# Rotary embedding on one core: the first slab's load in one piece instead of eight, and the stores issued by GpSimd's software ring instead of ScalarE's hardware ring

## The chip, the core and the metric

The kernel runs on one core of a Trainium2 chip. The time is device microseconds (us) of one execution of the whole program. The profile comes from one further execution under the hardware profiler, with its own time.

## The reference

The kernel applies rotary position embedding to `x`, shape (16, 512, 1024) in float32, seen as 16 heads of 64 numbers. With `x1` and `x2` the two halves of a head and `cos`, `sin` of shape (512, 32), shared by all batches and heads:

```python
x = x.reshape(batch, seq, num_heads, head_dim)
x1, x2 = x[..., :half_dim], x[..., half_dim:]
rotated = concatenate([x1 * cos - x2 * sin,
                       x1 * sin + x2 * cos], axis=-1)
```

Input and output are 33.55 MB each, so 67.1 MB pass through the DMA engines, plus 0.13 MB of tables.

## The kernel before, in words

The 16 batches are cut into eight **slabs** of two batches. A slab is 128 partitions by 8192 float32, so one partition holds one contiguous run of 32 KB in HBM, and one slab is 4.19 MB. Five slab buffers (`slots = 5`) lie in SBUF. Slab `s + 5` is loaded into the buffer of slab `s`, once the store of slab `s` has landed.

All loads are issued by SyncE (SP), in its hardware ring: slabs 1 to 7 by `load` (L62), each as one DMA over 128 partitions. The first slab is loaded by a loop of its own (L68): eight DMAs, and DMA number `p` writes partitions p, p+8, p+16 and so on, 16 of them, 32 KB each. GpSimd (POOL) issues the two table loads (L78) in its software ring and builds a selection matrix. TensorE and VectorE (DVE) make from it a bfloat16 table `tab` in which cos and sin stand in the order of the slab.

The work is done in **passes**. For slabs 0 to 5 a pass is the whole slab; slabs 6 and 7 are cut into two passes of half a slab. Below, 6a and 6b are the halves of slab 6, and 7a and 7b those of slab 7. A pass has these steps:

1. ScalarE (ACT) casts the slab to bfloat16, `xb` (`cast`, L120). Two `xb` buffers exist.
2. DVE multiplies twice and adds once (L140 twice, L143); the products with sin go into the slab's own buffer.
3. ACT casts `xb` back to float32 into the slab (L146).
4. After a slab's last pass, ACT issues the store of the whole slab as one DMA (L148), in ACT's own hardware ring. Then the load of slab `s + 5` is put into SP's queue.

The source writes the input cast of pass `i + 1` ahead of the DVE work of pass `i`. The framework's scheduler settles the order on each engine from the program, and each engine runs its queue strictly in order. At the end of this kernel ACT's queue is: input cast 7a, output cast 6b, input cast 7b, store 6, output cast 7a, output cast 7b, store 7.

The framework gives DMAs of the hardware rings eight completion semaphores in turn, and those of the software ring eight others. A DMA whose semaphore is still in use waits at issue until the earlier DMA has landed.

Of the kernel before, what the change touches and what calls it, by code (L numbers as in the profile page):

```python
# [2 lines left out]

# [4 lines left out]


@with_exitstack  # L10
def kernel(
    ctx: ExitStack,
    tc: tile.TileContext,
    x: bass.AP,
    cos: bass.AP,
    sin: bass.AP,
    num_heads: int,
    out: bass.AP,
):
    nc = tc.nc  # L20
    P = nc.NUM_PARTITIONS

    batch, seq, dim = x.shape
    nh = num_heads
    hd = dim // nh
    half = hd // 2
    bf16 = mybir.dt.bfloat16
    f32 = mybir.dt.float32

    nb = 2  # L30
    slots = 5
    nslabs = batch // nb
    rpp = nb * seq // P
    W = rpp * dim
    SP = seq // rpp
    TW = rpp * half

    out_flat = out.rearrange("b s h d -> b s (h d)")

    singles = ctx.enter_context(tc.tile_pool(name="singles", bufs=1))  # L40
    slabs = ctx.enter_context(tc.tile_pool(name="slabs", bufs=slots))
    xpool = ctx.enter_context(tc.tile_pool(name="xpool", bufs=2))
    psum = ctx.enter_context(tc.tile_pool(
        name="psum", bufs=1, space=bass.MemoryType.PSUM))


    def dram(t, s, a=0, n=W):
        return bass.AP(tensor=t.tensor, offset=t.offset + s * nb * seq * dim + a,
                       ap=[[W, P], [1, n]])


    def view(t, offset, *dims):
        return dataclasses.replace(t, offset=t.offset + offset,
                                   ap=[t.ap[0], *[list(d) for d in dims]])


    slab = {}


    def load(s):  # L60
        slab[s] = slabs.tile([P, W], f32, tag="slab", name="slab")
        nc.sync.dma_start(out=slab[s], in_=dram(x, s))  # L62

    slab[0] = slabs.tile([P, W], f32, tag="slab", name="slab")
    for p in range(P // 16):
        nc.sync.dma_start(  # L68
            out=slab[0][p::P // 16, :],
            in_=bass.AP(tensor=x.tensor, offset=x.offset + p * W,  # L70
                        ap=[[P // 16 * W, 16], [1, W]]))


    TR = seq // P
    G = rpp // TR
    raw = singles.tile([P, 2 * TR * half], f32, tag="raw")
    for i, src in enumerate((cos, sin)):
        nc.gpsimd.dma_start(out=view(raw, i * TR * half, (1, TR * half)), in_=bass.AP(  # L78
            tensor=src.tensor, offset=src.offset,
            ap=[[TR * half, P], [1, TR * half]]))  # L80

    for s in range(1, slots):
        load(s)


    pick = singles.tile([P, G * P], bf16, tag="pick")
    nc.gpsimd.memset(pick, 0.0)  # L87
    for g in range(G):
        part = view(pick, g * P, (SP, P // SP), (1, SP))
        nc.gpsimd.affine_select(  # L90
            out=part, in_=part, compare_op=mybir.AluOpType.not_equal, fill=1.0,
            base=-g, pattern=[[0, P // SP], [-G, SP]], channel_multiplier=1)

    tab1 = singles.tile([P, 2 * TR * half], bf16, tag="tab1")
    nc.vector.tensor_copy(out=tab1, in_=raw)  # L95
    acc = psum.tile([P, 2 * TW], f32, tag="acc")
    for i in range(2):
        for g in range(G):
            nc.tensor.matmul(view(acc, i * TW + g * TR * half, (1, TR * half)),  # L99
                             view(pick, g * P, (1, P)),  # L100
                             view(tab1, i * TR * half, (1, TR * half)),
                             start=True, stop=True)

    tab = singles.tile([P, 2 * rpp * hd], bf16, tag="tab")
    nc.vector.tensor_copy(out=view(tab, 0, (hd, 2 * rpp), (1, half)),  # L105
                          in_=view(acc, 0, (half, 2 * rpp), (1, half)))
    nc.vector.tensor_copy(out=view(tab, half, (hd, rpp), (1, half)),  # L107
                          in_=view(acc, 0, (half, rpp), (1, half)))
    nc.vector.tensor_scalar_mul(  # L109
        out=view(tab, rpp * hd + half, (hd, rpp), (1, half)),  # L110
        in0=view(acc, TW, (half, rpp), (1, half)), scalar1=-1.0)

    xb = {}


    def cast(u):
        s, r, n = u
        if r == 0:
            xb[s] = xpool.tile([P, W], bf16, tag="xb", name="xb")
        nc.scalar.copy(out=view(xb[s], r * dim, (1, n * dim)),  # L120
                       in_=view(slab[s], r * dim, (1, n * dim)))

    passes = []
    for s in range(nslabs):
        n = rpp if s < nslabs - 2 else rpp // 2
        passes += [(s, r, n) for r in range(0, rpp, n)]


    cast(passes[0])
    for i, (s, r, n) in enumerate(passes):
        if i + 1 < len(passes):
            cast(passes[i + 1])
        xs = view(slab[s], r * dim, (1, n * dim))
        xu = view(xb[s], r * dim, (1, n * dim))

        t2 = view(slab[s].bitcast(bf16), 2 * r * dim, (1, n * dim))
        for t, a in ((t2, rpp * hd), (xu, 0)):
            nc.vector.tensor_mul(  # L140
                out=t, in0=xu,
                in1=view(tab, a + r * hd, (hd, n), (0, nh), (1, hd)))
        nc.vector.tensor_add(  # L143
            out=xu, in0=xu, in1=view(t2, half, (hd, n * nh), (-half, 2), (1, half)))

        nc.scalar.copy(out=xs, in_=xu)  # L146
        if r + n == rpp:
            nc.scalar.dma_start(out=dram(out_flat, s), in_=slab[s])  # L148
            if s + slots < nslabs:
                load(s + slots)  # L150


# [1 line left out]
_INS = ['x', 'cos', 'sin', 'num_heads']  # L154
_OUTS = [((16, 512, 16, 64), 'float32')]

_NUMBERS = {'num_heads': 16}


# [26 lines left out]
```

## Time and profile before

| | |
|---|---|
| median of 3 runs | 171.97 us (171.81 to 172.14) |
| the profiled execution | 171.81 us, of which the profile's span is 170.0 us |
| ACT busy | 113.5 us (67%) |
| DVE busy | 108.7 us (64%) |
| POOL busy | 2.3 us (1%) |
| DMA | 67.24 MB, mean 395 GB/s over the span |

The span runs from the first instruction to the last event of the program; about 1.8 us of the execution's time lie outside it. The page cuts the span into 40 slices of 4.25 us, and gives for each the busy share of the 16 DMA engines and what they moved. The busy share of an engine's packets says that packets were in work, not how fast; the line of GB/s under it does.

### The profile page before, as it was taken

The page shows a single profiled execution, that of the slowest core. Times are in us where ns is not written, and L with a number is a line of the kernel's source. Part 1 is how long each engine was busy: PE and PEld are TensorE (multiplying, and loading weights), DVE is VectorE, ACT ScalarE, POOL GpSimd, SP SyncE. Part 2 cuts the span into 40 slices and gives each one's busy share as a digit, 9 for nine tenths or more (in the row PEclk, how much of TensorE's full clock was granted, in tenths as well). Part 3 has the DMA queues.
Part 4 walks back from the last instruction along what each step waited for, and adds up shares of the span by engine and source line. Part 5 has one row for each costly group of instructions (what it writes and reads, how often), then busy time and mean ns, then how long its engine had stood idle before and what let it go on. Part 6 is the DMA issues. An engine that isn't in the chain of part 4 may idle for free.

```text
span 170.0 us, 169 instructions
## 1 busy us (share of the span) xinstructions
PE 0.6 (0%) x4; PEld 0.4 (0%) x4; DVE 108.7 (64%) x34; ACT 113.5 (67%) x21; POOL 2.3 (1%) x9
## 2 busy tenths in 40 slices
PE   0010000000000000000000000000000000000000
PEld 0000000000000000000000000000000000000000
DVE  0030000399999889979979997994965959980000
ACT  0000039695298999999999999908999599917000
POOL 5000000000000000000000000000000000000000
DMA  5989979999999999999999898989898989898985
GB/s 133 268 185 193 239 285 455 409 455 409 455 409 455 409 455 432 432 439 424 463 401 478 385 486 378 486 378 486 378 486 378 486 378 486 378 493 378 486 378 239
DMA packets 2480, 67.24 MB, mean 395 GB/s; under 512 B 400, under 2 KB 400, under 8 KB 432
## 3 DMA queue, kind: packets, MB, share of 16 engines
q1 hardware_dynamic: 1264, 33.56, 52.0%
q10 hardware_dynamic: 1152, 33.55, 45.7%
q0 software_dynamic: 64, 0.13, 0.4%
HBM read 33.69 MB, written 33.55 MB: 395 GB/s over the span
## 4 chain that ended last, share of the span: by engine, by line
DMA 42%; ACT 33%; DVE 12%; SPq 2%; issue 2%; ACTq 0%
DMA slab<-in_x_dram 27%; ACT slab L146 17%; ACT xb L120 15%; DMA out_dram<-slab 15%; DVE xb L143 4%; DVE slab L140 4%; DVE xb L140 4%; SPq L68 2%; ACT L120 1%; ACTq L148 0%; ACTq L120 0%; ACTq L146 0%; SPq L62 0%
## 5 line engine op out<-in xcount | busy, mean ns | idle before, releaser
L120 ACT CAST xb<-slab 128x8192 bf16<-128x8192 f32 (+1 forms) x10 | 56.5, 5652 | 10.0 <-DMA slab<-in_x_dram 8.7
L146 ACT CAST slab<-xb 128x8192 f32<-128x8192 bf16 (+1 forms) x10 | 56.5, 5650 | 8.6 <-DVE xb L143 8.6
L140 DVE TENSOR_TENSOR slab<-xb,tab 128x8192 bf16<-128x8192 bf16 (+1 forms) x10 | 35.7, 3571 | 33.0 <-ACT xb L120 32.9
L143 DVE TENSOR_TENSOR xb<-xb,slab 128x8192 bf16<-128x8192 bf16 (+1 forms) x10 | 35.7, 3572 | 0.3
L140 DVE TENSOR_TENSOR xb<-xb,tab 128x8192 bf16<-128x8192 bf16 (+1 forms) x10 | 35.7, 3571 | 0.3
L120 ACT ACT_TABLE_LOAD x1 | 1.3, 1283 | 24.0 <-DMA slab<-in_x_dram 24.0
L95 DVE CAST tab<-raw 128x256 bf16<-128x256 f32 x1 | 0.3, 294 | 9.3 <-DMA raw<-in_sin_dram 9.3
L105 DVE CAST tab<-acc 128x512 bf16<-128x512 f32 x1 | 0.7, 692 | 0.7 <-PE acc L99 0.7
L78 POOL DMA_DIRECT2D raw<-in_cos_dram x1 | 0.7, 674 | 0.8 <-POOLq L167 0.8
L99 PE MATMUL acc<-tab,pick 128*128 128x128 bf16 x4 | 0.6, 299 | 9.6 <-DVE tab L95 9.6
L78 POOL DMA_DIRECT2D raw<-in_sin_dram x1 | 0.5, 534 | 0.0
L90 POOL TENSOR_SCALAR_AFFINE_SELECT pick<-pick 128x128 bf16<-128x128 bf16 x2 | 0.5, 288 | 0.1
L99 PEld LDWEIGHTS <-pick 128*128 128x128 bf16 x4 | 0.4, 126 | 9.5 <-issue 6.3
L109 DVE TENSOR_SCALAR tab<-acc 128x256 bf16<-128x256 f32 x1 | 0.4, 416 | 0.0
L107 DVE CAST tab<-acc 128x256 bf16<-128x256 f32 x1 | 0.4, 415 | 0.0
L87 POOL MEMSET pick<- 128x256 bf16 x1 | 0.3, 330 | 0.0
L167 POOL MEMSET const-bfloat16-1.0<- 128x1 bf16 x1 | 0.1, 102 | 0.0
L167 POOL MEMSET const-uint8-127<- 128x1 uint8 x1 | 0.1, 102 | 0.0
L167 POOL MEMSET const-float32-0.0<- 128x1 f32 x1 | 0.1, 98 | 0.2 <-issue 0.2
L167 POOL MEMSET const-float32-1.0<- 128x1 f32 x1 | 0.1, 98 | 0.0
## 6 DMA issues: line engine op xcount, KB each, us to landing
out_dram<-slab ACTq DMA_DIRECT2D x8, 4096.0 KB, 22.4
slab<-in_x_dram SPq DMA_DIRECT2D x7, 4096.0 KB, 27.4
slab<-in_x_dram SPq DMA_DIRECT2D x8, 512.0 KB, 12.4
raw<-in_cos_dram POOLq DMA_DIRECT2D x1, 64.0 KB, 5.1
raw<-in_sin_dram POOLq DMA_DIRECT2D x1, 64.0 KB, 7.3
```

What stands on the lines that cost most here:

```text
L68: nc.sync.dma_start(out=slab[0][p::P // 16, :], in_=bass.AP(tensor=x.tensor, offset=x.offset + p * W, ap=[[P // 16 * W, 16], [1, W]]))
L78: nc.gpsimd.dma_start(out=view(raw, i * TR * half, (1, TR * half)), in_=bass.AP(tensor=src.tensor, offset=src.offset, ap=[[TR * half, P], ...
L90: nc.gpsimd.affine_select(out=part, in_=part, compare_op=mybir.AluOpType.not_equal, fill=1.0, base=-g, pattern=[[0, P // SP], [-G, SP]], c ...
L99: nc.tensor.matmul(view(acc, i * TW + g * TR * half, (1, TR * half)), view(pick, g * P, (1, P)), view(tab1, i * TR * half, (1, TR * half)) ...
L105: nc.vector.tensor_copy(out=view(tab, 0, (hd, 2 * rpp), (1, half)), in_=view(acc, 0, (half, 2 * rpp), (1, half)))
L107: nc.vector.tensor_copy(out=view(tab, half, (hd, rpp), (1, half)), in_=view(acc, 0, (half, rpp), (1, half)))
L109: nc.vector.tensor_scalar_mul(out=view(tab, rpp * hd + half, (hd, rpp), (1, half)), in0=view(acc, TW, (half, rpp), (1, half)), scalar1=-1.0)
L120: nc.scalar.copy(out=view(xb[s], r * dim, (1, n * dim)), in_=view(slab[s], r * dim, (1, n * dim)))
L140: nc.vector.tensor_mul(out=t, in0=xu, in1=view(tab, a + r * hd, (hd, n), (0, nh), (1, hd)))
L143: nc.vector.tensor_add(out=xu, in0=xu, in1=view(t2, half, (hd, n * nh), (-half, 2), (1, half)))
L146: nc.scalar.copy(out=xs, in_=xu)
L167: nc = _bacc.Bacc("TRN2", target_bir_lowering=False, num_devices=1)
```

## The change

The loop of eight DMAs for the first slab is replaced by `load(0)`, one DMA over 128 partitions like those of the other slabs. And the store of a finished slab is issued by GpSimd, in the software ring, instead of by ScalarE in its hardware ring. The sizes and the order of the stores stay as they are.

```diff
-    slab[0] = slabs.tile([P, W], f32, tag="slab", name="slab")
-    for p in range(P // 16):
-        nc.sync.dma_start(
-            out=slab[0][p::P // 16, :],
-            in_=bass.AP(tensor=x.tensor, offset=x.offset + p * W,
-                        ap=[[P // 16 * W, 16], [1, W]]))
+    load(0)
...
         nc.scalar.copy(out=xs, in_=xu)
         if r + n == rpp:
-            nc.scalar.dma_start(out=dram(out_flat, s), in_=slab[s])
+            nc.gpsimd.dma_start(out=dram(out_flat, s), in_=slab[s])
             if s + slots < nslabs:
                 load(s + slots)
```

In the changed program the scheduler also orders the last casts otherwise. ACT's queue now runs: input casts 6a and 6b, output cast 5, input cast 7a, output casts 6a and 6b, input cast 7b, output casts 7a and 7b. The eight stores follow GpSimd's own setup work in its queue. SP's queue is eight loads, the first five of them without a wait.

## The prediction

> **What bounds the kernel now.** I read the page's slices first, because both rings share 16 DMA engines.
>
> ```profile
> DMA  5989979999999999999999898989898989898985
> GB/s 133 268 185 193 239 285 455 409 455 409 455 409 455 409 455 432 432 439 424 463 401 478 385 486 378 486 378 486 378 486 378 486 378 486 378 493 378 486 378 239
> ```
>
> The engines have packets in work all the time, but in the first six slices (25.5 us) they move about half of what they move later. The table by stage puts it in figures; its last two columns are the DMA share and GB/s.
>
> ```profile
> 4.25:24.00 19.75, 0.58 (x4) 0.31 (x3) 1.65 (x4) 0.04 (x1) 0.00 (x0) 1.00 1.01 220
> 24.00:28.00 4.00, 0.00 (x0) 0.00 (x0) 0.00 (x0) 3.99 (x2) 0.00 (x0) 1.00 1.06 459
> 134.00:146.00 12.00, 0.00 (x0) 0.00 (x0) 9.85 (x6) 11.28 (x4) 0.00 (x0) 1.00 1.01 437
> ```
>
> 220 GB/s against about 433 in the long run (29 us from 24 to 53 show 433). The queue lines confirm it over the whole run: loads (q1) and stores (q10) carry the same bytes, but the loads took 52.0% against 45.7% of the engines' time. 6.3% of 170.0 us is 10.7 us lost, all with the first slab.
>
> ```profile
> q1 hardware_dynamic: 1264, 33.56, 52.0%
> q10 hardware_dynamic: 1152, 33.55, 45.7%
> q0 software_dynamic: 64, 0.13, 0.4%
> ```
>
> The chain in order of time says when that slab landed (5.23 + 18.64 = 23.87), and when the last load did (107.47 + 27.23 = 134.70). All compute hangs on the first, the tail on the second.
>
> ```profile
> 5.23 18.64 DMA slab<-in_x_dram
> ...
> 107.47 27.23 DMA slab<-in_x_dram
> ```
>
> From 24 us on the engines move at the same full rate to the end. So the kernel is a slow first load and then 63 MB at 433 GB/s. ACT (113.5 us) and DVE (108.7 us) bind only where they hold back the last store. The timeline of the tail shows how narrow that is; columns are start, duration, engine and line.
>
> ```profile
> 134.72 3.60 ACT L120 CAST xb<-slab 128x4096 bf16<-128x4096 f32 x1 [1.81 <-DMA slab<-in_x_dram]
> 138.23 3.60 ACT L146 CAST slab<-xb 128x4096 f32<-128x4096 bf16 x1
> ...
> 141.74 3.60 ACT L120 CAST xb<-slab 128x4096 bf16<-128x4096 f32 x1
> ...
> 145.37 2.29 DVE L140 TENSOR_TENSOR slab<-xb,tab 128x4096 bf16<-128x4096 bf16 x1
> ...
> 152.40 3.60 ACT L146 CAST slab<-xb 128x4096 f32<-128x4096 bf16 x1 [3.46 <-DVE xb L143]
> 156.04 0.34 ACTq L148 DMA_DIRECT2D out_dram<-slab  x1
> ```
>
> Store 7 is issued 21.3 us after the last load landed. The packet records have its first packet at 158.47 and the end of its data at 168.73; store 6 keeps the engines busy until then. It came in time by a hair.
>
> **Part 1, the first slab in one piece.** Its 128 packets of 32 KB took 2.47 us each (packet records); those of the other loads take 1.22, the stores' 1.21. As one DMA like slab 1's it should move at 433 GB/s: 4.19 MB / 433 = 9.7 us. Packets begin at 2.08 us now, and the issue at 0.74 does not move. The tables' packets cost 0.4% of the span, 0.65 us per engine; I put 0.3 us of that into this stretch. Last packet to landing is 0.35 us (168.73 to 169.08). So slab 0 lands at 2.1 + 9.7 + 0.3 + 0.3 = 12.4 instead of 23.87: **11.5 us earlier**. The seven issues that go away (0.57 to 0.68 us each) ran beside transfers and bring nothing. The waits of SP's queue on early loads (14.4 us in five waits, one hardware semaphore each) also go away, since the stores leave these semaphores; they hid behind queued packets and bring nothing either. The tables are ready at 11.6 now; DVE first needs them at 12.4 + 1.3 (table load of ACT) + 7.0 = 20.7, so a later arrival by a few us is covered.
>
> Does the gain reach the end? Slabs 1 to 4 follow at 9.7 us each, to 51 us. Store 0 is issued 28.9 us after slab 0 landed (23.87 to 52.79), so at 41.3: before the loads run dry. From there on, loads and stores alternate as before, all of it 11.5 us earlier, and the last load lands at 134.7 - 11.5 = 123.2. With everything shifted the span would be 158.5 and the time 160.3.
>
> **Part 2, ACT's order.** Eight store issues leave ACT: 7 x 0.34 + 0.38 = 2.8 us, of an engine that idles a third of the time; nothing on the end, except that the scheduler now places output cast 6a behind input cast 7a. After the last load: input cast 7a 3.6, output casts 6a and 6b 3.5 each (138.23 to 141.74 is one step), input cast 7b 3.5, three DVE steps 7.0, output cast 7b 3.6, with the handovers 24.8 us instead of 21.3. DVE used to start 7b at once behind 7a; now it waits 3.5 us for input cast 7b. So store 7 is issued at 123.2 + 24.8 = 148.0, whereas store 6's data are out at 159.0 - 11.5 = 147.5. The hair is gone: what is late next is store 7.
>
> **Part 3, the software ring.** GpSimd has nothing else to do after 3.4 us (the last step of its setup), so a store waits for no other instruction on it but the store ahead. Three costs:
> - *Issue to first packet.* Before, 1.34 us on idle engines in the hardware ring (0.74 to 2.08), and 2.6 us in the software ring on busy ones (the table load, 1.25 to 3.86). For stores 0 to 6 it lies beside transfers. For store 7 it is on the path. I take 2.0, between the two, as the engines are then idle but the ring is the software one; ends 1.3 and 4.0 (the wait of store 0 among loads, 52.79 to 56.75).
> - *Rate.* Low end: the hardware store's packets, 1.21 us per 32 KB, nothing added. High end: the only software packets here, 4 KB in 0.25 to 0.37 us, eight for a row, 2.0 us at the least. With 64 packets per engine that adds 64 x 0.8 = 51 us. I take the low end: a table packet gathers eight pieces of 512 B, while a row of the slab is one run of 32 KB on both sides, as in the hardware ring.
> - *Descriptors beside DVE.* The only two software issues ran (1.25 to 2.45) before DVE's first instruction at 9.28, so the trace doesn't show them together. Low end nothing. If an issue waits for the running DVE instruction, up to 4.4 us: store 0 then goes at 45.7, still before 51, and store 7 meets an idle DVE: nothing. High end: held until DVE pauses, three instructions, 13.3 us: store 0 goes at 54.6, with the engines dry from 51 on and load 5 as late; about 7 us at the end. I take nothing.
>
> [...]
>
> **The sum.** Store 7 issued 148.0, first packet 150.0, 9.7 of data, 0.35 to the landing, 0.95 from there to the span's end (169.08 to 170.03 before): 161.0. Outside the span lie 1.8: **162.8** for an execution like the profiled one, whose 171.81 lies 0.16 under the median; I forecast 162.9.
>
> **The rivals.**
> - *Saturated to the end* (0.20): the rings don't share evenly, loads get more, and the last load lands early enough for store 7. For it: nothing in the page shows how a software ring shares with a hardware one. 160.3.
> - *Held by DVE* (0.15): as above, 163 to 170.
> - *Slower: software packets stay dear* (0.08). If a row goes out as 4 KB packets at the table's 0.25 us, the stores cost 51 us more: 162.9 + 51 = about 214. It turns the sign from 9.1 us / 64 = 0.14 us more per 32 KB, that is 1.35 us instead of 1.21.
> - *The slow start is the start's, not the form's* (0.03): then part 1 gives nothing, and the new order adds 3.5: about 175. Against it: the rate doubles exactly as the first slab ends.
>
> **How the numbers follow.** The forecast has 0.50, the rivals 0.46, and 0.04 is left for what I don't see. Faster: 0.50 + 0.20 + 0.15 and half of the rest, 0.87; slower 0.11; within 0.2%, about what a measurement here can tell from no change, 0.02. The range takes in the saturated case from below, and from above the 4 us issue and most of the holding by DVE: 160.0 to 168.5.
>
> **What would show it.** Right: slices at 430 GB/s from the second on; slab 0 landed near 12.4; store 0 issued near 41; q1's share about equal to that of the stores; one dip of about 2 us before store 7. Wrong: store packets well over 1.21 us, issues on GpSimd that last several us, or a dry stretch around 51 us.

## The result, and the profile after

The changed kernel takes 164.45 us (median of 4 runs, 163.93 to 165.38) against 172.06 before: a ratio of 0.957, with a 95% interval of 0.952 to 0.961. The forecast was 162.9 with a range of 160.0 to 168.5. The profiled execution took 164.35 us, its span is 162.6.

The page of the changed kernel, its slices and its queues. `q0`, the software ring, now carries the tables and all stores:

```profile
DMA  7999989989989999999999999989989989995993
GB/s 258 403 403 460 443 387 476 427 387 484 419 379 395 419 476 395 451 443 395 460 435 395 500 395 395 508 387 443 460 387 460 443 387 484 419 395 258 387 484 161
...
q1 hardware_dynamic: 1152, 33.55, 48.7%
q0 software_dynamic: 1216, 33.69, 48.0%
```

The slow six slices at the start are gone. Loads and stores now cost the engines nearly the same, 48.7% and 48.0%, where it was 52.0% and 45.7%. One slice near the end, 258 GB/s, is new. The table by stage has the same stretch at the start as the one shown of before, and the hole at the end:

```profile
4.25:24.00 19.75, 0.58 (x4) 0.32 (x3) 5.31 (x5) 8.01 (x2) 0.00 (x0) 1.00 1.00 431
...
150.00:152.00 2.00, 0.00 (x0) 0.00 (x0) 0.00 (x0) 0.00 (x0) 0.53 (x1) 1.00 0.61 262
```

431 GB/s instead of 220. The timeline of the tail shows the hole's cause (L114 and L140 are the input and output cast in this kernel, L120 and L146 before):

```profile
124.91 3.60 ACT L114 CAST xb<-slab 128x4096 bf16<-128x4096 f32 x1 [5.33 <-DMA slab<-in_x_dram]
128.42 7.11 ACT L140 CAST slab<-xb 128x4096 f32<-128x4096 bf16 x2
...
135.44 3.60 ACT L114 CAST xb<-slab 128x4096 bf16<-128x4096 f32 x1
...
139.07 2.29 DVE L134 TENSOR_TENSOR slab<-xb,tab 128x4096 bf16<-128x4096 bf16 x1 [3.58 <-ACT xb L114]
...
146.10 3.60 ACT L140 CAST slab<-xb 128x4096 f32<-128x4096 bf16 x1 [3.56 <-DVE xb L137]
150.00 0.53 POOL L142 DMA_DIRECT2D out_dram<-slab  x1 [13.64 <-ACT slab L140]
```

Slab 7's second half waits for its input cast (135.44), which stands behind two output casts of slab 6; DVE idles 3.58 us for it. Store 7 is issued at 150.0, 25.2 us after the last load landed at 124.8; before it was 21.3. The packet records (start, length and size of every DMA packet in the trace) have the last data of store 6 at 149.89 and the first of store 7 at 151.09: the engines stand still for 1.2 us. Before, store 7's first packet (158.47) came ahead of the last data of store 6 (159.05).

### The profile page after: what moved, and what is told of

The parts are those of the page before. It is cut to its first block, busy times and chain, and to the rows that moved or that the text cites. A ratio compares the mean times of both kernels' runs of the same rounds, so it can differ in the third digit from the quotient of the medians.

```text
span 162.6 us, 163 instructions
## 1 busy us (share of the span) xinstructions
PE 0.6 (0%) x4; PEld 0.4 (0%) x4; DVE 108.4 (67%) x34; ACT 113.4 (70%) x21; POOL 6.6 (4%) x17
## 3 DMA queue, kind: packets, MB, share of 16 engines
q1 hardware_dynamic: 1152, 33.55, 48.7%
## 4 chain that ended last, share of the span: by engine, by line
DMA 35%; issue 30%; ACT 17%; DVE 8%; POOL 1%; POOLq 0%; ACTq 0%; SPq 0%
DMA slab<-in_x_dram 22%; DMA out_dram<-slab 13%; ACT xb L114 9%; ACT slab L140 9%; DVE xb L137 3%; DVE slab L134 3%; DVE xb L134 3%; POOL out_dram L142 1%; POOLq L175 0%; POOLq L142 0%; ACTq L114 0%; SPq L62 0%; ACTq L140 0%
## 5 line engine op out<-in xcount | busy, mean ns | idle before, releaser
L114 ACT CAST xb<-slab 128x8192 bf16<-128x8192 f32 (+1 forms) x10 | 56.4, 5652 | 28.3 <-DMA slab<-in_x_dram 28.2
L140 ACT CAST slab<-xb 128x8192 f32<-128x8192 bf16 (+1 forms) x10 | 56.4, 5650 | 7.3 <-DVE xb L137 7.3
L142 POOL DMA_DIRECT2D out_dram<-slab x8 | 4.3, 538 | 142.8 <-ACT slab L140 142.8
```

The lines of the kernel that those rows point to most:

```text
L114: nc.scalar.copy(out=view(xb[s], r * dim, (1, n * dim)), in_=view(slab[s], r * dim, (1, n * dim)))
L142: nc.gpsimd.dma_start(out=dram(out_flat, s), in_=slab[s])
```

## The experiments

**The two edits apart.** The theory was that the first slab's form brings the gain, and that the changed order of ACT's casts, not the software ring, gives a part of it back. The rival was that the ring costs. The first run (e1) leaves the stores with ACT (the scheduler then keeps the old order of the casts):

```diff
+    load(0)            # in place of the loop of eight DMAs
...
             nc.scalar.dma_start(out=dram(out_flat, s), in_=slab[s])
```

> The first slab in one piece, stores left with ScalarE in the hardware ring. The scheduler then keeps the old order of the last casts. Theory (the new order of casts is what the changed kernel loses): slab 0 lands near 13.3 as in the changed kernel, everything behind it is the profile of before moved by 10.6 us (23.87 - 13.26), no pause before store 7: 171.8 - 10.6 = 161.2 us. Rival (the software ring itself costs the changed kernel its 3 us): the same 161.2 here, so this run sets the mark. If the first slab's form were not the cause of the slow start: 172.

Measured: 162.5 us (161.71 to 163.99), ratio 0.949 (0.943 to 0.955). That is 1.3 us above the 161.2 of both theories, whose sum has no dip (see below); the profiled execution took 161.76. Slab 0 lands at 13.6 and the last load at 124.1; store 7 goes out at 145.4, 21.3 us later as before, and its first packet, at 148.65, comes before the last data of store 6 are out at 149.10: no pause. The second run (e2) has only the other edit:

```diff
-            nc.scalar.dma_start(out=dram(out_flat, s), in_=slab[s])
+            nc.gpsimd.dma_start(out=dram(out_flat, s), in_=slab[s])
```

> Stores by GpSimd, the first slab still in eight DMAs of every eighth partition. The scheduler then has the new order of the last casts. Both theories: the last load lands near 134.7, store 7 is issued 25.2 us later at 159.9, 1.1 to its first packet, 9.9 of data, 1.6 to the end of the span: 172.5, and with 1.8 outside it 174.3 us, 2.3 slower than before. Held by DVE (descriptors wait for DVE's pauses): 177 or more. No cost of the stores at all: 172.

Measured: 173.81 us (173.44 to 174.0), ratio 1.0115 (1.0099 to 1.0132). So the stores' edit by itself makes the kernel 1.2% slower (expected 174.3), and the whole gain comes from the first slab. The last load landed at 133.9, store 7 went out at 159.08, 25.2 us later: the term expected.

**Ring or order.** The changed kernel with the old order of the casts (e3); the input cast is held in the same way:

```diff
...
-        nc.scalar.copy(out=xs, in_=xu)
+        tc.keep_in_program_order(nc.scalar.copy(out=xs, in_=xu))
```

> The changed kernel with ACT's casts held in the order of the source, which is that of before (cast 6a, output cast 5, cast 6b, output cast 6a, cast 7a, output cast 6b, cast 7b, output casts 7a and 7b). Theory: store 7 is issued 21.6 us after the last load instead of 25.2, at 146.4, so there is no pause and the time falls by 2 to 3 us to 161.2 to 162.2. Rival (the software ring itself costs it): the order was not what mattered, 164.2 to 164.6.

Measured: 162.69 us (162.2 to 163.53), ratio 0.948 (0.944 to 0.951). The software ring is kept and most of the loss is gone; the time stands 0.5 us above the range of the theory and 1.5 below that of the rival, and the last load landed 1.3 us later than in the changed kernel. The tail of its timeline: input cast 7b starts 7.0 us after 7a instead of 10.5, and store 7 is issued 21.6 us after the last load (126.1) instead of 25.2.

```profile
126.15 3.60 ACT L114 CAST xb<-slab 128x4096 bf16<-128x4096 f32 x1 [1.83 <-DMA slab<-in_x_dram]
129.67 3.60 ACT L141 CAST slab<-xb 128x4096 f32<-128x4096 bf16 x1
...
133.17 3.60 ACT L114 CAST xb<-slab 128x4096 bf16<-128x4096 f32 x1
...
147.73 0.53 POOL L143 DMA_DIRECT2D out_dram<-slab  x1 [13.64 <-ACT slab L141]
```

Next, only the last store goes back to ACT's ring, with the new order (e4):

```diff
+            eng = nc.scalar if s == nslabs - 1 else nc.gpsimd
+            eng.dma_start(out=dram(out_flat, s), in_=slab[s])
```

> The changed kernel with only the last store issued by ScalarE in its hardware ring; the new order of casts stays. Theory: issue to first packet was 1.1 us in the software ring and was 1.3 in the hardware ring on idle engines, and 0.3 us of handover from ACT to GpSimd falls away: 164.1 to 164.6, no change that shows. Rival (the software ring's way from issue to data and to landing is what costs): 1 to 2 us less, 162.5 to 163.5.

Measured: 163.91 us (163.23 to 165.25), ratio 0.955 (0.950 to 0.960), the same as the changed kernel within the intervals. The interval just reaches that of the run before, so the time alone decides little. In its packet records the hardware store's first packet comes 0.9 us after its issue, against 1.1 in the software ring: the two rings hardly differ there.

The fourth corner of the square has the stores by ACT with the new order (e10). The first edit alone is run once more beside it (e11). The main lines of the edit:

```diff
-        if i + 1 < len(passes):
-            cast(passes[i + 1])
+        for j in {5: (6, 7), 6: (8,), 7: (), 8: (9,), 9: ()}.get(i, (i + 1,)):
+            cast(passes[j])
```

> As e1_load_only (first slab in one piece, stores by ScalarE), but ACT's casts are held in the changed kernel's order (6a and 6b ahead of output cast 5, 7a ahead of output casts 6a and 6b). With e1, e3 and the changed kernel this makes the square of two rings and two orders. Theory (the order alone costs, the ring nothing): store 7 is issued 25 us after the last load instead of 21.3, a pause of 1 to 2 us comes ahead of it, and the time is 1.5 to 2.5 us over e1: ratio to before 0.955 to 0.962, as the changed kernel. Rival (order costs only together with the software ring): as e1, ratio 0.945 to 0.951.

> The kernel of e1_load_only again, on the same chip as e10_scalar_stores_new_order and with more rounds, to have the difference between the two orders and a narrower interval for the fastest kernel. Theory: 161.7 to 163.5, ratio 0.943 to 0.951, 1.5 to 2.5 us under e10. Rival: the same as e10.

Measured: 164.62 us (163.18 to 165.55 in five executions; a sixth took 165.92) and 162.32 us (162.19 to 163.21). As ratios to before:

| stores by | old order of casts | new order of casts |
|---|---|---|
| ACT, hardware ring | 0.945 (0.943 to 0.947) | 0.957 (0.954 to 0.961) |
| GpSimd, software ring | 0.948 (0.944 to 0.951) | 0.957 (0.952 to 0.961) |

Down the columns there is nothing that the intervals can tell apart; across the rows the new order costs about 1%, 1.5 to 2.1 us. The first set of e1, 0.949 (0.943 to 0.955), is too wide to show this by itself. With ACT's ring too, the new order issues store 7 late, 25.3 us after the last load had landed at 124.5:

```profile
124.51 3.60 ACT L114 CAST xb<-slab 128x4096 bf16<-128x4096 f32 x1 [5.34 <-DMA slab<-in_x_dram]
...
149.84 0.34 ACTq L143 DMA_DIRECT2D out_dram<-slab  x1
```

The first edit alone thus has the lowest median, 162.3 us in the second set; the run with the software ring and the old order can't be told from it. Both beat before and after.

**Why the first slab was slow.** The theory was that what counts is which partitions one DMA writes. Two kernels like before have other sets of partitions in the first slab's DMAs. Sixteen neighbours each (e6):

```diff
-            out=slab[0][p::P // 16, :],
+            out=slab[0][16 * p:16 * p + 16, :],
...
```

> The kernel before, but each of the first slab's eight DMAs writes 16 neighbouring partitions (0 to 15, 16 to 31 and so on) instead of every eighth; number, size and queue of the DMAs stay. [...] Rival (eight DMAs of 16 rows are slow as such): slab 0 landed near 23.9 as before, 172 us.

And four DMAs of every fourth partition (e7):

```diff
-    for p in range(P // 16):
+    for p in range(4):
...
-            out=slab[0][p::P // 16, :],
+            out=slab[0][p::4, :],
...
```

> The kernel before, but the first slab is loaded by four DMAs of every fourth partition, 32 partitions each. [...] Rival (DMAs with stepping partitions, or several of them, are slow as such): slab 0 landed between 18 and 24, 166 to 172 us.

Measured, one execution each: 188.41 us, 16.4 above the 172 of the rival, and 163.41 us, 2.6 below the rival's range. The slices and the load queue of the first, then the load queue of the second:

```profile
GB/s 112 112 126 126 112 112 112 112 232 442 449 449 449 449 372 414 449 449 450 449 435 379 421 449 449 449 449 428 372 435 449 449 449 449 428 372 435 449 449 225
...
q1 hardware_dynamic: 1264, 33.56, 56.2%
```

```profile
q1 hardware_dynamic: 1200, 33.56, 49.2%
```

The first slab's packets (32 KB, as everywhere) take 4.44 us with 16 neighbours, 2.47 with every eighth, 1.29 with every fourth, 1.28 with all 128 partitions in one DMA; slab 0 lands at 40.4, 23.9, 14.0 and 13.3. Eight DMAs of the same size differ by a factor of nearly two with the set of partitions, and four stepping ones are as fast as one. So neither the number of eight nor the stepping explains the slow start by itself. Two things are not separated: partition p always holds row p of HBM, so the rows read change with the partitions written, and no run has DMAs of 16 rows that are fast. The rates in the packet records are about 114 GB/s for 16 neighbours, 210 for every eighth and 432 for every fourth partition and for all 128. What in the chip sets these rates is not shown.

**A dip that the prediction did not have.** In the packet records of the changed kernel the rate falls to 303, 271 and 404 GB/s in the three microseconds from 44 on, about 0.8 us lost. Before, with the slow first slab, has no such dip: its store 0 is issued at 52.79, and each microsecond from 52 to 66 moves 431 to 434 GB/s. Two runs went after it, both with ACT's ring, one execution each. The first (e8) has slab 0 in two halves, so that its store goes earlier:

```diff
+    for a in (0, W // 2):
+        nc.sync.dma_start(out=view(slab[0], a, (1, W // 2)), in_=dram(x, 0, a, W // 2))
...
-        n = rpp if s < nslabs - 2 else rpp // 2
+        n = rpp if 0 < s < nslabs - 2 else rpp // 2
```

> Load in one piece and stores by ScalarE, as in e1_load_only, but slab 0 is loaded in two DMAs of half the columns and worked on in two halves, so that its store is issued some 8 us earlier, near 33. All theories: the same time as e1_load_only, 161.7 to 164, as the DMA engines are the bound. It places the dip that the traces of whole loads show at 44 to 46 us (rate down to 300 GB/s for 2 us, 3 us after the first store's issue). If the dip belongs to the first store's arrival among five queued loads: it moves to 35 to 38. If it belongs to the time or to load 4: it stays at 44 to 46.

Measured: 162.86 us. Store 0 is issued at 29.9, and the dip stands at 32 to 36 (394, 332, 337 and 404 GB/s). It moved with the first store. It is not the software ring's: with ACT's ring e1 moves 360 GB/s from 43 to 47, and e10 356 in the slice from 44.5 to 48.5; with the software ring e3 moves 344 from 43 to 47. The main lines of the other run (e9), which also holds the order of ACT's casts and stores:

```diff
+    nc.gpsimd.tensor_copy(out=view(slab[slots - 1], 0, (1, 1)), in_=view(slab[0], 0, (1, 1)))
+    nc.sync.dma_start(out=slab[slots - 1], in_=dram(x, slots - 1))   # slab 4
```

> As e1_load_only, but the load of slab 4 is issued only when slab 0 has landed (a one-column GpSimd copy from slab 0 into slab 4's buffer holds it back; the load overwrites it), near 14 instead of 2.4, so that at most four loads are queued at once. The order of ScalarE's queue is that of the source, as in e1. All theories: same time as e1_load_only, 161.7 to 164. If the dip at 44 to 46 comes from the fifth load's descriptors waiting long in the ring: it is gone. If from the first store or the time: it stays.

Measured: 177.7 us, and it answers another question than the one asked. In this program the scheduler orders DVE's work otherwise: the passes of slabs 0 and 1 ran interleaved, and store 0 went out at 63.6 instead of 41.1. Its slices:

```profile
GB/s 238 390 474 410 425 469 387 454 454 387 469 238 0 0 238 358 358 335 358 380 477 417 417 454 425 432 447 387 477 440 395 454 440 417 447 410 454 358 477 238
```

By the packet records no data move from 51.6 to 64.5: all five slots are loaded and none is free. There is no dip at 44 to 46; the slice from 44.0 to 48.4 moves 469 GB/s. The slow stretches from 74 to 83 are a gap with load 5 starting behind it, and a dip that begins 2 us after store 1's issue (77.95). The dip thus begins after the issue of a store that joins queued loads, and before that store's first packet. In e7 store 0 is issued at 42.9 and its first packet comes at 47.7, while the rate is 351, 261, 289 and 351 GB/s from 44 to 48. The long packets are those of the loads, up to 2.7 us instead of 1.21 (2.55 in load 4 of the changed kernel). Before lets a store join queued loads too (store 0's first packet comes at 56.75, and load 4's packets run until 67.07) and has no dip. What causes it stays open.

## Why the prediction was right, point by point

*First slab in one piece.* Right in kind: it landed 10.6 us earlier instead of 11.5. The chain of the changed kernel in order of time:

```profile
0.74 12.52 DMA slab<-in_x_dram
13.26 0.02 issue
13.29 7.03 ACT xb L114
...
41.09 21.67 DMA out_dram<-slab
```

Slab 0 lands at 13.26, not 12.4. The mis-sized term is the 9.7 us at 433 GB/s from the first packet on: in the packet records the first two full microseconds move 246 and 337 GB/s. The sum had no row for such a start, as the slow form stays below these rates anyway (at most 229 GB/s in a microsecond of its first eight). Store 0 went at 41.1 (41.3 expected), well before the loads run dry (load 4's packets end at 58.4). One reason given in passing was wrong: the waits of SP's queue on early loads do not go because the stores leave its semaphores. They are still there with the stores by GpSimd alone (e2, 14.2 us in six waits) and gone with the first edit alone (e1), as in the changed kernel, where SP waits for no load; so it was the eight DMAs that filled the semaphores.

*The shift of the rest.* The last load landed at 124.8, not 123.2: 0.9 comes from the start, and the other 0.7 is about the size of the dip, for which the sum had no term.

*ACT's order.* Right: 25.2 us from last load to store 7 for an expected 24.8, of which some 0.3 is the handover from ACT to GpSimd (cast ended 149.70, issue 150.0). That the order and not the ring costs is shown by the square above.

*The software ring.* Packets of the stores took 1.21 us per 32 KB, the low end that the sum took: a row went out as one packet. The rival of dear packets falls. Its price was also too high. The tables' 4 KB packets, 0.25 to 0.37 us before, take 0.16 in every kernel with a fast first slab and 0.61 beside the slowest one (16 neighbours), so the slow first slab had made them dear; eight of them at 0.16 make 1.27 us, an estimate that would add about 4 us and not 51. Issue to first packet was 1.1 us for store 7, below the 1.3 that was the low end; 2.0 was taken. No long hold by DVE shows. GpSimd's own group:

```profile
L142 POOL DMA_DIRECT2D out_dram<-slab x8: 531/531/568, 41.1 to 150.0; - x8
```

Store 0 was issued in the middle of a DVE multiplication (38.05 to 42.47) in 0.57 us, store 7 with DVE idle in 0.53. The first packet of store 0 came 4.9 us after its issue, among the loads, against 4.6 for the same store in the hardware ring (e1); with the slow first slab it was 3.7 (e2) against 4.0 (before). This rules out the high end of 13.3 us. A wait for the end of the running multiplication, 1.4 us here, could hide behind the loads, and only the length of the issue speaks against it. Every DVE instruction beside a store here is a `TENSOR_TENSOR`; these runs show nothing of others. What a late store 0 costs is seen roughly in e9, where DVE's order differs too: 22 us late, 15 us more than e1.

*The sum.* Term by term against 161.0 for the span: last load +1.6, to the issue +0.4, issue to packet -0.9, data (9.9) +0.2, from landing to the end of the span (1.22) +0.3. That is +1.6, and the span measured was 162.6. So the likeliest case was the one that happened, with some luck in the size: the 0.9 taken too much for the issue hid more than half of what the late last load cost. The condition of the saturated rival, an earlier last load, did not come. Its figure, 160.3, is that of a kernel without the reordering: such kernels took 161.8 and 162.2 in their profiled executions (e1, e11), above it by about the slow start and the dip.

## What to carry to other kernels

When two rings share the DMA engines, compare their shares of time for the same bytes: 52.0% against 45.7% pointed at the gain, and busy slices hid it. A DMA's rate changed here with the partitions that it names, so a first tile like this one is better split by columns (162.86 us) or by every fourth partition (163.41) than by every eighth (172.06) or by blocks of 16 neighbours (188.41). Moving an issue to another engine can let the scheduler reorder the engine that it left; look at the order around the last transfer, as two casts in front of one input cast cost more here (1.5 to 2.1 us) than the ring, for which the intervals show nothing.

## What the runs showed of the hardware that was not expected

The transfer starts slowly even in full form, 246 and 337 GB/s in its first two full microseconds in the changed kernel. Loads and stores together move 433 GB/s from 57 to 133 us before, with the stores in the hardware ring, and 434 from 47 to 123 in the changed kernel, with the stores in the software ring. With a fast first slab the rate dips for two to four microseconds (303, 271 and 404 GB/s from 44 on in the changed kernel; 394, 332, 337 and 404 from 32 on in e8); the dip begins between the first store's issue and its first packet (41.09 and 45.98 in the changed kernel), and its cause is open. So is that of the wider spread of their times: 161.71 to 163.99 us in the first set of e1, against 171.64 to 172.01 before on the same chip. Small packets of the software ring took longer beside a slow slab in the other ring: 4 KB took 0.16, 0.33 and 0.61 us beside DMAs of all partitions, every eighth and 16 neighbours.
